# A feed-forward's gate and up products of raw rows, with the norm's factor multiplied in behind them

## The chip, the core and the metric

The kernel runs on one core of a Trainium2 chip. Its time is the device time of one execution in microseconds (us). The core has a matrix engine (PE), a vector engine (DVE), a scalar engine (ACT), a general engine (POOL, also called GpSimd) and an engine that issues transfers (SP). Each engine works through its own list of instructions in order and waits at the head of the list for what the next one needs.

## What is computed

One step of a layer with two feed-forwards around a token mixer. The parts that matter here:

```python
def rms_norm(x, g):
    xf = x.astype(F32)
    y = xf * lax.rsqrt(jnp.mean(xf * xf, axis=-1, keepdims=True) + EPS)
    return (y * g.astype(F32)).astype(x.dtype)

def swiglu(x, w1, w2):
    gate, up = jnp.split(x @ w1, 2, axis=-1)
    return (jax.nn.silu(gate) * up) @ w2
...
        x = x + 0.5 * swiglu(rms_norm(x, lp["norm_ffn1"]), lp["ffn1_w1"], lp["ffn1_w2"])
        y, ns = token_mixing(rms_norm(x, lp["norm_mix"]), lp, st, sample)
        x = x + y
        x = x + 0.5 * swiglu(rms_norm(x, lp["norm_ffn2"]), lp["ffn2_w1"], lp["ffn2_w2"])
```

There are 656 columns (16 meta, 512 prompt and 128 sample tokens; 640 in the second feed-forward), 1024 features and 2816 inner features. The norm's factor, one over the root of a column's mean square, is called R. R belongs to a column, so x's products with the weights may be made of rows without R, and multiplied by R afterwards.

## The kernel before

x lies as eight row tiles of 128 features by 656 columns. The inner features are 22 chunks of 128, in groups of 5, 5, 4, 4 and 4. For each chunk the gate's and the up part's products are made, then the chunk's output v; after a group the second weight matrix's products are added to x, one of eight output tiles o after another (`x<-mx,x` or `x<-mm,x` in the trace).

Every 32-bit operand is split in a high and a low part, and each product is made of three (high by high, high by low, low by high). ACT makes the high part of a weight piece (`whi<-wraw`, `whi<-wsum`), DVE the low part (`wlo<-...`): a piece has four tiles of 128x128. A ring of five such pieces (RING) stands between them and the matrix engine; `more` refills it after each product. The raw weights come through two buffers `wraw`.

The first three chunks (CLASSIC) are plain: 8 row tiles x 3 parts x gate and up x 2 column halves are 96 matmuls. Their operands are raw rows: `gained` makes the high and the low part of gain times x. `act` (lines 696 to 705) multiplies the gate's product with R on DVE (`hg<-mm,R`), takes the tanh on ACT, and two more DVE instructions and one of POOL (`row<-hs,R`) make v.

The other 19 chunks go through `chunk7`, which makes a chunk's four blocks of products (gate and up, two column halves) with seven products of 12 matmuls in place of eight, 84 in all, of sums of weight blocks and of sums of rows. The weight sums are four instructions of POOL for each chunk (`wsum<-...`). The sums of rows are made in `sums_in`, of rows that are normalised first (`row<-x,par,R` is x times gain times R), in pieces between chunks 0 to 2. Here the gate's product needs no R. A chunk's products end in four accumulators p1, p5, p6 and p7; DVE adds a first sum u to two of them (`mx<-mx,u`) before further products are added into the same bank. Behind the gate's tanh an instruction of DVE (`hg<-hs,mx`: tanh in SBUF, gate in PSUM) and one product (`row<-hg,up` or `row<-hg,mx`) write v. Then ACT makes v's high part (`f<-row`) and DVE its low part (`f<-row,f`).

R comes from `row_scale`: the sums of squares of x (`acc`), a matmul with ones, ten small DVE instructions (`nrow`, `rsy`, `rsq`), and a matmul that spreads the result over the partitions (`mx<-sqc,nrow`).

A scheduler sets each engine's list from the program's order and from its own picture of when operands are there; the lists are fixed when the kernel is built. All instructions are recorded with the line of one helper, L188, so the names of the tiles tell them apart. Buffer numbers are left out in the trace's names.

Of the kernel before, what the change touches and what calls it, by code (L numbers as in the profile page):

```python
# [24 lines left out]
CLASSIC = 3  # L25
RING = 5
# [201 lines left out]
class Kern:  # L228
# [366 lines left out]
    def sums_in(self, x, gain, c0, n, slots):  # L595


        nc = self.nc
        V, G, S = nc.vector, nc.gpsimd, nc.scalar
        H, E, _ = slots  # L600
        Y, Z, X, Q = self.pairs(H[:8]), self.pairs(H[8:]), self.pairs(E[:8]), self.pairs(E[8:])
        lo_, hi_ = slice(0, n), slice(n, 2 * n)

        def rows(k):
            r = self.row()[:, :2 * n]
            V.scalar_tensor_tensor(r, x[:, k, c0:c0 + 2 * n], self.p(gain, k), self.R[:, c0:c0 + 2 * n],
                                   op0=OP.mult, op1=OP.mult)
            return r

        def split(dst, cols, src):  # L610
            h, l = (t[:, cols] for t in dst)
            S.activation(h, src, AF.Copy)
            V.tensor_tensor(l, src, h.bitcast(F32), OP.subtract)

        both = slice(0, 2 * n)
        for j in range(4):
            a, b, z = rows(j), rows(j + 4), self.row()[:, both]
            V.tensor_tensor(z[:, hi_], b[:, hi_], a[:, hi_], OP.subtract)
            V.tensor_tensor(a[:, hi_], a[:, hi_], a[:, lo_], OP.subtract)
            V.tensor_tensor(z[:, lo_], b[:, hi_], a[:, hi_], OP.subtract)  # L620
            split(Y[j], both, a)
            split(Z[j], both, z)
        yield
        for j in range(4):
            b, q = rows(j + 4), self.row()[:, lo_]
            split(X[j], both, b)
            G.tensor_tensor(q, b[:, lo_], Z[j][0][:, lo_].bitcast(F32), OP.subtract)
            G.tensor_tensor(q, q, Z[j][1][:, lo_].bitcast(F32), OP.subtract)
            split(Q[j // 2], (lo_, hi_)[j % 2], q)
# [1 line left out]
        self.xc = {"11": part(Y, lo_), "t1": part(Y, hi_), "t2": part(Z, lo_), "t3": part(Z, hi_),
                   "21": part(X, lo_), "22": part(X, hi_),
                   "t4": [[t[:, (lo_, hi_)[j % 2]] for t in Q[j // 2]] for j in range(4)]}
        yield
# [1986 lines left out]
```

## Time and profile before

| what | value |
| --- | --- |
| runs | 1557.96, 1564.41 (median), 1564.84 us |
| profiled execution | 1560.96 us, of it a span of 1559.0 us |
| PE busy | 1463.2 us, 94% |
| DVE busy | 1050.1 us, 67% |
| ACT, POOL busy | 601.4, 459.5 us |
| mean granted clock of PE | 0.962 |

The span runs from the first to the last instruction of the profiled execution; busy shares are averages over the whole span. The granted clock is a share of full speed: 1.00 is 2.4 GHz and 0.50 is 1.2 GHz, and a value between them is a stretch with both.

### The profile page before, as it was taken

The page shows a single profiled execution, that of the slowest core. Times are in us where ns is not written, and L with a number is a line of the kernel's source. Part 1 is how long each engine was busy: PE and PEld are TensorE (multiplying, and loading weights), DVE is VectorE, ACT ScalarE, POOL GpSimd, SP SyncE. Part 2 cuts the span into 40 slices and gives each one's busy share as a digit, 9 for nine tenths or more (in the row PEclk, how much of TensorE's full clock was granted, in tenths as well). Part 3 has the DMA queues.
Part 4 walks back from the last instruction along what each step waited for, and adds up shares of the span by engine and source line. Part 5 has one row for each costly group of instructions (what it writes and reads, how often), then busy time and mean ns, then how long its engine had stood idle before and what let it go on. Part 6 is the DMA issues. An engine that isn't in the chain of part 4 may idle for free.

```text
span 1559.0 us, 26349 instructions
## 1 busy us (share of the span) xinstructions
PE 1463.2 (94%) x10171; PEld 1361.9 (87%) x10171; DVE 1050.1 (67%) x2118; ACT 601.4 (39%) x1142; POOL 459.5 (29%) x580
## 2 busy tenths in 40 slices
PE   7789999999999989999987999989989999999996
PEld 7789999999999757878776877789879999999996
DVE  7985857676775266764765555775995775858586
ACT  5343524343453252454423323233442443434351
POOL 3323314141303333222432523411251313131310
PEclk9889999999999998999888999999989999999998
DMA  8122231313124101212367343473013222222221
GB/s 260 36 68 82 72 105 55 109 55 108 55 88 156 59 35 37 82 59 80 109 202 204 97 109 106 126 242 119 28 44 105 75 76 82 82 82 82 82 82 68
DMA packets 106348, 148.14 MB, mean 95 GB/s; under 512 B 20128, under 2 KB 67760, under 8 KB 106224
## 3 DMA queue, kind: packets, MB, share of 16 engines
q1 hardware_dynamic: 103088, 143.99, 29.2%
q10 hardware_dynamic: 3136, 2.47, 0.6%
q8 instruction: 80, 1.31, 0.4%
q14 instruction: 44, 0.36, 0.1%
HBM read 119.88 MB, written 26.56 MB: 94 GB/s over the span
## 4 chain that ended last, share of the span: by engine, by line
PE 76%; DVE 12%; POOL 4%; issue 3%; DMA 3%; ACT 2%; SPq 1%; DVEq 0%; ACTq 0%; POOLq 0%
PE mx L188 59%; PE mm L188 17%; DVE row L188 2%; DVE wlo L188 1%; DVE e L188 1%; DMA r<-in_w_out 1%; DVE x L188 1%; DVE n L188 1%; DVE hg L188 1%; POOL row L188 1%; POOL qh L188 1%; DVE P L188 1%; SPq L188 1%; DVE rsq L188 0%; DVE f L188 0%
## 5 line engine op out<-in xcount | busy, mean ns | idle before, releaser
L188 ACT ACTIVATE whi<-wraw 128x512 fp32r<-128x512 f32 (+2 forms) x260 | 169.4, 653 | 321.7 <-PE mx L188 195.6
L188 PE MATMUL mx<-f,whi 128*128 128x384 f32 (+2 forms) x1220 | 262.5, 309 | 2.1 <-ACT f L188 2.1
L188 POOL TENSOR_TENSOR wsum<-wraw 128x512 f32<-128x512 f32 x76 | 111.6, 1469 | 451.7 <-DMA wraw<-in_f1w 143.1
L188 DVE TENSOR_TENSOR wlo<-wraw,whi 128x512 fp32r<-128x512 f32 (+1 forms) x227 | 193.5, 853 | 62.9 <-ACT whi L188 62.2
L188 PE MATMUL mm<-n,whi 128*128 128x400 f32 (+2 forms) x992 | 206.6, 329 | 3.9 <-DVE raw L188 2.1
L188 PE MATMUL mx<-e,whi 128*128 128x320 f32 (+4 forms) x996 | 187.0, 317 | 13.3 <-ACT e L188 8.4
L188 PEld LDWEIGHTS mx<-f,whi 128*128 128x128 f32 x1220 | 195.6, 189 | 2.3 <-ACT f L188 2.3
L188 PEld LDWEIGHTS mx<-e,whi 128*128 128x128 f32 x996 | 159.0, 193 | 17.5 <-ACT e L188 9.9
L188 PEld LDWEIGHTS mm<-n,whi 128*128 128x128 f32 x992 | 160.5, 196 | 13.1 <-issue 5.3
L188 PE MATMUL mx<-n,whi 128*128 128x320 f32 (+1 forms) x992 | 169.8, 314 | 0.0
L188 ACT ACTIVATE whi<-wsum 128x512 fp32r<-128x512 f32 x152 | 95.7, 629 | 154.4 <-PE mx L188 112.9
L188 PEld LDWEIGHTS mx<-n,whi 128*128 128x128 f32 x992 | 154.5, 191 | 0.2 <-ACT whi L188 0.2
L188 PE MATMUL mx<-f,wlo 128*128 128x384 f32 (+2 forms) x610 | 152.1, 308 | 0.0
L188 DVE TENSOR_TENSOR wlo<-wsum,whi 128x512 fp32r<-128x512 f32 x152 | 110.6, 729 | 54.9 <-ACT whi L188 54.3
L188 PE MATMUL mm<-n,wlo 128*128 128x400 f32 (+1 forms) x496 | 120.7, 325 | 1.0 <-DVE wlo L188 0.6
L188 POOL TENSOR_TENSOR wlo<-wraw,whi 128x1024 fp32r<-128x1024 f32 (+1 forms) x31 | 67.1, 2173 | 147.7 <-ACT whi L188 104.8
L188 PE MATMUL mx<-e,wlo 128*128 128x320 f32 (+4 forms) x498 | 105.1, 316 | 3.9 <-DVE wlo L188 3.9
L188 DVE SCALAR_TENSOR_TENSOR x<-mx,x 128x256 f32<-128x256 f32 (+2 forms) x130 | 60.9, 483 | 62.9 <-PE mx L188 62.2
L188 PEld LDWEIGHTS mx<-f,wlo 128*128 128x128 f32 x610 | 99.8, 189 | 0.0
L188 PE MATMUL mx<-n,wlo 128*128 128x320 f32 (+1 forms) x496 | 94.3, 312 | 0.4 <-DVE wlo L188 0.4
L188 PE MATMUL mm<-f,whi 128*128 128x400 f32 (+1 forms) x284 | 89.0, 330 | 5.8 <-ACT f L188 5.8
L188 PEld LDWEIGHTS mx<-e,wlo 128*128 128x128 f32 x498 | 82.6, 193 | 4.1 <-DVE wlo L188 4.1
(592 smaller groups left out, 2652.2 us busy)
## 6 DMA issues: line engine op xcount, KB each, us to landing
wraw<-in_f2w SPq DMA_DIRECT2D x22, 1024.0 KB, 5.0
wraw<-in_f1w SPq DMA_DIRECT2D x21, 1024.0 KB, 5.0
wraw<-in_w_in SPq DMA_DIRECT2D x24, 512.0 KB, 3.7
wraw<-in_f1w SPq DMA_DIRECT2D x12, 512.0 KB, 3.6
wraw<-in_f2w SPq DMA_DIRECT2D x12, 512.0 KB, 3.6
scr_rw<-kx SPq DMA_DIRECT2D x16, 328.0 KB, 2.8
wraw<-in_f1w SPq DMA_DIRECT2D x8, 640.0 KB, 4.0
wraw<-in_f2w SPq DMA_DIRECT2D x8, 640.0 KB, 3.9
```

What stands on the lines that cost most here:

```text
L188: return f(*a, **k)
```

## The change

All products of both feed-forwards are now made of raw rows (gain times x, without R). Only chunk 0 stays plain (`chunk0`); chunks 1 to 21 go through `chunk7`. The sums of rows are made of raw rows and column half by column half, in the first feed-forward as the row tiles arrive (`halves_of`, `sums_of`), for which the tiles are loaded in the order 0, 4, 1, 5, 2, 6, 3, 7. R is multiplied in behind the products: in `gate`, on DVE, into the gate's product, and in `gated`, on POOL, into v. The ring of weight pieces goes from five to six, the buffers of row tiles from five to four.

```diff
-CLASSIC = 3
-RING = 5
+ROWS = (0, 4, 1, 5, 2, 6, 3, 7)
+RING = 6
...
-        return self.t(self.fv, [128, NT], "row", bufs=5)
+        return self.t(self.fv, [128, NT], "row", bufs=4)
...
+    def halves_of(self, x, gain, k, hs=(0, 1)):
+
+        c0, n = self.half
+        todo = [("2", 0, 2)] if k > 3 and len(hs) == 2 else [(("11", "12", "21", "22")[k // 4 * 2 + h], h, 1) for h in hs]
+        for name, h, w in todo:
+            hi, lo = self.xc[name][k % 4]
+            v, g = x[:, k, c0 + h * n:c0 + (h + w) * n], self.p(gain, k)
+            self.nc.scalar.activation(hi, v, AF.Copy, scale=g)
+            self.nc.vector.scalar_tensor_tensor(lo, v, g, hi.bitcast(F32), op0=OP.mult, op1=OP.subtract)
+
+    def sums_of(self, x, gain, j):
...
+        S.activation(g12, b12, AF.Copy, scale=g)
+        V.scalar_tensor_tensor(m1, b11, g, g12, op0=OP.mult, op1=OP.subtract)
+        V.scalar_tensor_tensor(t2, b22, g4, m1, op0=OP.mult, op1=OP.add)
+        V.scalar_tensor_tensor(t3, b22, g4, g12, op0=OP.mult, op1=OP.subtract)
+        t4 = g12
+        V.scalar_tensor_tensor(t4, b21, g4, t2, op0=OP.mult, op1=OP.subtract)
+        for name, v, s in (("t23", b[:, :2 * n], 1.0), ("t1", m1, -1.0), ("t4", t4, 1.0)):
+            hi, lo = self.xc[name][j]
+            S.activation(hi, v, AF.Copy, scale=s)
+            V.scalar_tensor_tensor(lo, v, s, hi.bitcast(F32), op0=OP.mult, op1=OP.subtract)
...
-        def gate(pg):
...
-            S.activation(s, pg, AF.Tanh, scale=0.5)
-            V.scalar_tensor_tensor(g, s, 1.0, pg, op0=OP.add, op1=OP.mult)
-            return g
...
-        V.tensor_tensor(v[:, c0 + n:c0 + 2 * n], gate(p5), up1, OP.mult)
+        self.gated(v, self.gate(p5, 1), up1, 1)
...
-        V.tensor_tensor(v[:, c0:c0 + n], g0, p7, OP.mult)
+        self.gated(v, g0, p7, 0)
...
+    def gate(self, pg, h):
+
+        c0, n = self.half
+        g, s = (self.t(self.fv, [128, 328], t, bufs=2)[:, :n] for t in ("hg", "hs"))
+        self.nc.vector.tensor_tensor(g, pg, self.R[:, c0 + h * n:c0 + (h + 1) * n], OP.mult)
+        self.nc.scalar.activation(s, g, AF.Tanh, scale=0.5)
+        self.nc.vector.scalar_tensor_tensor(g, s, 1.0, g, op0=OP.add, op1=OP.mult)
+        return g
+
+    def gated(self, v, g, pu, h):
+        c0, n = self.half
+        c = slice(c0 + h * n, c0 + (h + 1) * n)
+        self.nc.vector.tensor_tensor(g, g, pu, OP.mult)
+        self.nc.gpsimd.tensor_tensor(v[:, c], g, self.R[:, c], OP.mult)
```

The lists of the engines show what the diff alone doesn't. In the list of PE in the opening of the first feed-forward, `mx<-one,acc` is the matmul of the sums of squares, `mx<-sqc,nrow` the one that spreads R, and whi and wlo are pieces of chunk 0 or 1. Before, with chunk 1 plain, fifteen matmuls of it stand ahead of R's; the last of them and what follows:

```order
L188 MATMUL mm100_435<-e421_109,whi69_339 128x256
L188 MATMUL mm100_435<-e522_110,whi69_339 128x256
L188 MATMUL mm100_435<-e421_109,wlo70_340 128x256
L188 MATMUL mx79_358<-sqc_68,nrow66_308 128x16
L188 MATMUL mx79_358<-sqc_68,nrow66_308 128x128 x3
L188 MATMUL mx80_364<-sqc_68,nrow66_308 128x128 x2
L188 MATMUL mx99_434<-f635_126,whi51_184 128x400
L188 MATMUL mx99_434<-f736_127,whi51_184 128x400
```

Now, where `mm101` is one product of chunk 1 (12 matmuls, the last of them shown) and `mx100` the next:

```order
L188 MATMUL mm101_461<-n1213_98,wlo66_261 128x328
L188 MATMUL mm101_461<-n1415_100,wlo66_261 128x328
L188 MATMUL mx79_377<-one_72,acc39_130 16x1
L188 MATMUL mx79_377<-one_72,acc39_130 128x1 x5
L188 MATMUL mx92_432<-sqc_68,nrow80_384 128x16
L188 MATMUL mx92_432<-sqc_68,nrow80_384 128x128 x3
L188 MATMUL mx93_438<-sqc_68,nrow80_384 128x128 x2
L188 MATMUL mx100_460<-n01_86,whi63_256 128x328
L188 MATMUL mx100_460<-n23_88,whi63_256 128x328
L188 MATMUL mx100_460<-n45_90,whi63_256 128x328
```

Chunk 1's other 72 matmuls, which need no R, have moved behind both of the norm's matmuls, and the matmul of the squares behind chunk 0.

In DVE's list of a chunk in the steady part, from the gate to the weight pieces of the next chunk, stood:

```order
L188 SCALAR_TENSOR_TENSOR hg344_1825<-hs343_1824,mx322_1724 128x328
L188 TENSOR_TENSOR wlo350_1850<-wsum333_1779,whi349_1849 128x512
L188 SCALAR_TENSOR_TENSOR hg348_1845<-hs347_1844,mx325_1727 128x328
L188 TENSOR_TENSOR row321_1723<-hg348_1845,up1340_1806 128x328
L188 TENSOR_TENSOR row321_1723<-hg344_1825,mx324_1726 128x328
L188 TENSOR_TENSOR wlo352_1867<-wraw300_1628,whi351_1866 128x512
L188 TENSOR_TENSOR f534_125<-row321_1723,f433_124 128x656
L188 TENSOR_TENSOR wlo360_1892<-wsum336_1782,whi359_1891 128x512
L188 TENSOR_TENSOR u2361_1907<-mx355_1874,c1358_1889 128x328
L188 TENSOR_TENSOR wlo363_1910<-wraw300_1628,whi362_1909 128x512
L188 TENSOR_TENSOR mm356_1875<-mm356_1875,u2361_1907 128x328
L188 TENSOR_TENSOR wlo370_1937<-wraw332_1777,whi369_1936 128x512
```

and now stands:

```order
L188 TENSOR_TENSOR hg365_1881<-mx343_1763,R91_431 128x328
L188 TENSOR_TENSOR wlo368_1889<-wraw316_1643,whi367_1888 128x512
L188 SCALAR_TENSOR_TENSOR hg365_1881<-hs366_1882,hg365_1881 128x328
L188 TENSOR_TENSOR hg365_1881<-hg365_1881,up1358_1842 128x328
L188 TENSOR_TENSOR hg361_1860<-hg361_1860,mx342_1762 128x328
L188 TENSOR_TENSOR wlo370_1907<-wsum352_1801,whi369_1906 128x512
L188 TENSOR_TENSOR f534_125<-row339_1759,f433_124 128x656
L188 TENSOR_TENSOR wlo378_1932<-wraw316_1643,whi377_1931 128x512
L188 TENSOR_TENSOR u2379_1947<-mx373_1914,c1376_1929 128x328
L188 TENSOR_TENSOR wlo386_1960<-wraw348_1796,whi385_1959 128x512
L188 TENSOR_TENSOR mm374_1915<-mm374_1915,u2379_1947 128x328
L188 TENSOR_TENSOR wlo388_1977<-wsum382_1952,whi387_1976 128x512
```

The product with R (`hg<-mx,R`) is new, the instruction behind the tanh reads `hg` in SBUF where it read the gate in PSUM, and the low part of the output (`f534`) stands where it did, but now behind POOL's writing of `row339` and not behind DVE's own.

POOL's list of such a chunk was four weight sums:

```order
L188 TENSOR_TENSOR wsum365_1928<-wraw332_1777 128x512
L188 TENSOR_TENSOR wsum366_1929<-wsum365_1928,wraw332_1777 128x512
L188 TENSOR_TENSOR wsum367_1930<-wraw332_1777 128x512
L188 TENSOR_TENSOR wsum368_1931<-wraw332_1777,wsum366_1929 128x512
```

and is now, for the same chunk with its two products:

```order
L188 TENSOR_TENSOR wsum381_1951<-wraw348_1796 128x512
L188 TENSOR_TENSOR wsum382_1952<-wsum381_1951,wraw348_1796 128x512
L188 TENSOR_TENSOR wsum383_1953<-wraw348_1796 128x512
L188 TENSOR_TENSOR row339_1759<-hg365_1881,R91_431 128x328
L188 TENSOR_TENSOR row339_1759<-hg361_1860,R91_431 128x328
L188 TENSOR_TENSOR wsum384_1954<-wraw348_1796,wsum382_1952 128x512
```

Both products have moved in behind three of the four sums.

In the opening of the second feed-forward, the head of the norm's chain (`nrow<-mx`) stood in DVE's list right behind the raw halves (`f72`, `e12`, ... with x2 and the gain `par`):

```order
L188 SCALAR_TENSOR_TENSOR e52400_11804<-x2_10620,par_69,e42399_11803 128x256
L188 SCALAR_TENSOR_TENSOR e72402_11806<-x2_10620,par_69,e62401_11805 128x256
L188 SCALAR_TENSOR_TENSOR e92404_11808<-x2_10620,par_69,e82403_11807 128x256
L188 SCALAR_TENSOR_TENSOR e112406_11810<-x2_10620,par_69,e102405_11809 128x256
L188 TENSOR_SCALAR nrow2437_11918<-mx2436_11912 128x5
L188 TENSOR_SCALAR rsy2438_11920<-nrow2437_11918 128x5
```

and now stands behind the last of the sums of rows:

```order
L188 SCALAR_TENSOR_TENSOR n72402_11870<-row2458_12025,n62401_11869 128x320
L188 SCALAR_TENSOR_TENSOR row2458_12025<-x2_10712,par_69,row2459_12026 128x320
L188 SCALAR_TENSOR_TENSOR n152410_11878<-row2459_12026,n142409_11877 128x640
L188 SCALAR_TENSOR_TENSOR e112422_11902<-row2458_12025,e102421_11901 128x320
L188 TENSOR_SCALAR nrow2467_12074<-mx2466_12068 128x5
L188 TENSOR_SCALAR rsy2468_12076<-nrow2467_12074 128x5
```

The chain itself is the same; 24 rows of sums have moved in ahead of it.

## Rows read from the trace of the kernel before

**Rows 1.** Page: busy time of each engine; the chain that ended last, by engine.

```profile
PE 1463.2 (94%) x10171; PEld 1361.9 (87%) x10171; DVE 1050.1 (67%) x2118; ACT 601.4 (39%) x1142; POOL 459.5 (29%) x580
...
PE 76%; DVE 12%; POOL 4%; issue 3%; DMA 3%; ACT 2%; SPq 1%; DVEq 0%; ACTq 0%; POOLq 0%
```

**Rows 2.** Stretches: each engine's busy time and instructions, granted clock, DMA share, GB/s.

```profile
48.00:52.00 4.00, 0.00 (x0) 0.00 (x0) 4.00 (x7) 1.84 (x4) 0.00 (x0) 1.00 0.00 0
80.00:84.00 4.00, 2.15 (x8) 1.66 (x8) 4.00 (x4) 1.72 (x3) 3.86 (x3) 0.50 0.00 0
117.00:156.00 39.00, 39.00 (x262) 38.99 (x261) 21.61 (x37) 12.81 (x23) 15.40 (x11) 1.00 0.23 82
173.00:186.00 13.00, 13.00 (x88) 12.98 (x88) 12.22 (x18) 6.88 (x14) 5.71 (x4) 1.00 0.23 83
186.00:199.00 13.00, 12.86 (x86) 12.60 (x85) 9.46 (x19) 6.65 (x13) 0.00 (x0) 1.00 0.27 78
```

**Rows 3.** DVE in order of time: start, us, instruction, idle before it and its releaser.

```profile
179.37 0.48 DVE L188 TENSOR_TENSOR row<-hg,mx 128x328 f32<-128x328 f32 x1
...
181.08 1.93 DVE L188 TENSOR_TENSOR f<-row,f 128x656 fp32r<-128x656 f32 x1
182.93 0.68 DVE L188 TENSOR_TENSOR wlo<-wsum,whi 128x512 fp32r<-128x512 f32 x1
183.53 0.48 DVE L188 TENSOR_TENSOR u<-mx,c 128x328 f32<-128x328 f32 x1
183.94 1.65 DVE L188 TENSOR_TENSOR wlo<-wraw,whi 128x512 fp32r<-128x512 f32 x1
...
187.13 0.49 DVE L188 TENSOR_TENSOR mx<-mx,u 128x328 f32<-128x328 f32 x1
```

**Rows 4.** POOL in order of time, weight sums of the first feed-forward.

```profile
150.57 1.29 POOL L188 TENSOR_TENSOR wsum<-wraw 128x512 f32<-128x512 f32 x1 [5.76 <-DVE wlo L188]
...
177.81 1.28 POOL L188 TENSOR_TENSOR wsum<-wraw 128x512 f32<-128x512 f32 x1 [5.76 <-DMA wraw<-in_f1w]
...
180.57 1.74 POOL L188 TENSOR_TENSOR wsum<-wraw 128x512 f32<-128x512 f32 x1
...
263.67 1.77 POOL L188 TENSOR_TENSOR wsum<-wraw 128x512 f32<-128x512 f32 x1 [5.68 <-DMA wraw<-in_f1w]
```

**Rows 5.** ACT in order of time: copies of one product in two neighbouring chunks.

```profile
173.19 0.43 ACT L188 ACTIVATE c<-mx 128x328 f32<-128x328 f32 x1
...
185.81 0.43 ACT L188 ACTIVATE c<-mx 128x328 f32<-128x328 f32 x1
```

**Rows 6.** DVE groups by form, 120 to 460 us: busy, mean ns, idle before.

```profile
L188 DVE TENSOR_TENSOR row<-hg,up 128x328 f32<-128x328 f32 x17 | 14.1, 829 | 0.6
...
L188 DVE SCALAR_TENSOR_TENSOR hg<-hs,mx 128x328 f32<-128x328 f32 x26 | 12.7, 488 | 0.0
...
L188 DVE TENSOR_TENSOR row<-hg,mx 128x328 f32<-128x328 f32 x9 | 4.4, 489 | 0.4
```

**Rows 7.** DVE in order of time, opening of the first feed-forward.

```profile
5.81 0.90 DVE L188 SCALAR_TENSOR_TENSOR f<-x,par,f 128x656 fp32r<-128x656 f32 x1 [4.56 <-ACT f L188]
...
9.16 2.00 DVE L188 SCALAR_TENSOR_TENSOR e<-x,par,e 128x656 fp32r<-128x656 f32 x1 [1.09 <-ACT e L188]
...
30.39 0.57 DVE L188 TENSOR_TENSOR hg<-mm,R 128x400 f32<-128x400 f32 x1 [0.47 <-ACT R L188]
...
109.54 0.57 DVE L188 SCALAR_TENSOR_TENSOR x<-mx,x 128x400 f32<-128x400 f32 x1
```

**Rows 8.** POOL in order of time, same opening.

```profile
65.87 2.22 POOL L188 TENSOR_TENSOR row<-hs,R 128x400 f32<-128x400 f32 x2 [0.91 <-DVE hs L188]
```

**Rows 9.** DVE in order of time, opening of the second feed-forward.

```profile
1096.34 0.16 DVE L188 TENSOR_SCALAR nrow<-mx 128x5 f32<-128x5 f32 x1
...
1098.15 0.16 DVE L188 SCALAR_TENSOR_TENSOR nrow<-rsq,rsy 128x5 f32<-128x5 f32 x1
...
1180.83 0.89 DVE L188 SCALAR_TENSOR_TENSOR x<-mx,x 128x384 f32<-128x384 f32 x2
```

More of the change, by code (lines that the diff above doesn't have):

```diff
@@ L592, in more @@
             self.ring.append(p)
[L595 to L629, printed above, removed]
-        part = lambda ts, c: [[t[:, c] for t in p] for p in ts]
[L631 to L634, printed above, removed]
@@ L636, in chunk7, with operands @@
-    def chunk7(self, v, c0, n):
+    def operands(self, slots, c0, n):
+        H, E, F = slots
+        Y, Z, X, Q, W = (self.pairs(t) for t in (H[:8], H[8:], E[:8], E[8:], F[6:]))
+        lo, hi = slice(0, n), slice(n, 2 * n)
+        part = lambda ts, c: [[t[:, c] for t in p] for p in ts]
+        two = lambda ts: [[t[:, (lo, hi)[j % 2]] for t in ts[j // 2]] for j in range(4)]
+        self.xc = {"11": part(Y, lo), "t1": part(Y, hi), "t23": part(Z, slice(0, 2 * n)), "t2": part(Z, lo),
+                   "t3": part(Z, hi), "2": part(X, slice(0, 2 * n)), "21": part(X, lo), "22": part(X, hi),
+                   "t4": two(Q), "12": two(W)}
+        self.half = c0, n
@@ new lines, in sums_of @@
+    def sums_of(self, x, gain, j):
+        V, S = self.nc.vector, self.nc.scalar
+        c0, n = self.half
+        b11, b12, b21, b22 = (x[:, k, c0 + h * n:c0 + (h + 1) * n] for k in (j, j + 4) for h in range(2))
+        g, g4 = self.p(gain, j), self.p(gain, j + 4)
+        a, b = self.row(), self.row()
+        g12, m1, t2, t3 = a[:, :n], a[:, n:2 * n], b[:, :n], b[:, n:2 * n]
+        S.activation(g12, b12, AF.Copy, scale=g)
[8 more added lines that the diff above has]
+            V.scalar_tensor_tensor(lo, v, s, hi.bitcast(F32), op0=OP.mult, op1=OP.subtract)
@@ new lines, in gated, with chunk0, mm @@
+    def gated(self, v, g, pu, h):
+        c0, n = self.half
+        c = slice(c0 + h * n, c0 + (h + 1) * n)
+        self.nc.vector.tensor_tensor(g, g, pu, OP.mult)
+        self.nc.gpsimd.tensor_tensor(v[:, c], g, self.R[:, c], OP.mult)
+    def chunk0(self, v, scale, rows):
+        T = self.nc.tensor
+        n = self.half[1]
+        pg, pu = ([self.wide()[:, :n] for _ in range(2)] for _ in range(2))
+        ws = [self.take() for _ in range(4)]
+        wg, wu = ([[t[:, k] for t in w] for w in ws[i:i + 2] for k in range(4)] for i in (0, 2))
+        g = scale()
+        first = [True, True]
+        def mm(ps, w, k, h, parts, stop):
+            xh, xl = self.xc[("11", "12", "21", "22")[k // 4 * 2 + h]][k % 4]
+            for i in parts:
+                wt, xt = ((w[k][0], xh), (w[k][0], xl), (w[k][1], xh))[i]
+                T.matmul(ps[h], wt, xt, start=k == 0 and i == 0, stop=stop and i == parts[-1])
+        if rows:
+            for k in ROWS:
+                for p, w in ((pg, wg), (pu, wu)):
+                    for h in range(2):
+                        mm(p, w, k, h, (0, 1), False)
+            for p, w in ((pg, wg), (pu, wu)):
+                for k in ROWS:
+                    for h in range(2):
+                        mm(p, w, k, h, (2,), k == 7)
+                if p is pg:
+                    next(g)
+        else:
+            for h in range(2):
+                for p, w in ((pg, wg), (pu, wu)):
+                    for k in ROWS:
+                        mm(p, w, k, h, (0, 1, 2), k == 7)
+                    if h == 0 and p is pg:
+                        next(g)
+                for _ in g:
+                    pass
+        self.more()
+        for _ in g:
+            pass
+        for h in range(2):
+            self.gated(v, self.gate(pg[h], h), pu[h], h)
@@ L691, in ffn @@
+    def ffn(self, x, cols, scale, F, done=None, norm=None, also=None, rows=True):
         nc = self.nc
         c0 = cols[0][0]
[L693 to L705 removed]
@@ L2499, in last @@
                                                                          x[:, k - 1:k + 1, a:a + n])
[L2501 removed]
+            K.ffn(x, fcols, lambda: K.row_scale(acc, fb, fcols, False), F, norm=last, rows=False)
         pctx.close()
```

89 lines of the change are left out of this document (20 added, 69 removed).

## The prediction

> **What bounds the kernel now.** I read the page first. The matrix engine is busy 94% of the span, and it holds 76% of the chain that ended last; the vector engine (DVE) holds 12% [rows 1]. An average of this kind hides stages, so the stretches come next [rows 2]. From 117 to 156 us the matrix engine is busy for all of 39.00 us: there time is columns. In the opening of the first feed-forward it stands still for all of 48 to 52, and from 80 to 84 it works 2.15 of 4 us at a granted clock of 0.50, its lower level of 1.2 GHz, while DVE is busy 4.00 of 4 in both stretches [rows 2]. So both ends of the argument are there: fewer columns pay in the steady part, and in the opening whatever shortens or reorders DVE's list pays.
>
> The steady part is less free than its 39.00 suggests. In a chunk in which GpSimd (POOL) makes four weight sums, DVE is busy 12.22 of 13.00 us; in the next one, without POOL, 9.46 [rows 2]. The single instructions say where the difference sits. A low part of a weight piece takes 0.68 us alone, with 0.60 to the next start, and 1.65 beside a POOL sum; the low part of the chunk's output takes 1.93 [rows 3]. POOL's sums lie at 177.81 to 182.3 and DVE's long instructions lie in the same time [rows 3, 4]. The grouped rows tell which instructions suffer: `row<-hg,up`, both inputs in SBUF, has a mean of 829 ns; `row<-hg,mx` and `hg<-hs,mx`, one input in PSUM, have 489 and 488, their undisturbed price [rows 6]. A chunk of 84 products lasts 12.62 us on the matrix engine, from the copy at 173.19 to the next at 185.81 [rows 5], or 0.150 us for a product of 328 columns. The link between the two engines is the add `mx<-mx,u` at 187.13 [rows 3]: the product that follows it adds into the same bank, and in 186 to 199 the matrix engine loses 0.14 us, the first time loss of that group [rows 2]. The cover there is thus used up.
>
> **The change, part by part.** *Columns.* Chunks 1 and 2 of both feed-forwards go from 96 products to 84. 12 x 0.150 = 1.80 us a chunk in the first; at 320 columns (0.1465 a product) 1.76 in the second: 7.1 us in all, if the matrix engine is what bounds those chunks. In both openings it isn't, so I work these out as a whole.
>
> *Opening of the first feed-forward.* DVE's list up to the end of the sums of squares is, by the order: 32 instructions of 328 columns (0.41 apart, as from 183.53 to 183.94 [rows 3]), 8 of 656 and 7 adds of 656 (twice that), 7 weight pieces (0.60): 13.1 + 12.3 + 4.2 = 29.6 us. It begins at about 5.4, half a row earlier than the 5.81 of before, and waits about 1.1 for a row, as ahead of 9.16 [rows 7]. POOL's eleven instructions beside it (about 1.4 us each) cost what they cost in the steady chunk: 12.22 for 18 instructions against 9.46 for 19 is 3.3 us for 5.71 us of POOL, 0.57 per us [rows 2], so 9. The sum is 45.1. Then the chain of the norm, ten steps from 1096.34 to 1098.3 in the second feed-forward [rows 9], with a matmul ahead and one behind it about 3.5: 48.6, where now R is used first at 30.39 [rows 7]. Here lies the catch of the order: the matrix engine has the norm's two matmuls ahead of 72 of chunk 1's 84 products, though raw products no longer need the norm. It has done its 108 earlier products by about 38 and stands some 10 us. From 48.6: 72 products 10.8; 2.7 for some twenty of them at the lower clock, where 8 take 2.15 us [rows 2]; three chunks 37.9; 2.5 lost in their weight sums (below); the first output tile 30 x 0.150 = 4.5: 107.0 against the 109.54 of now [rows 7]. I take **-2.5**. Bounds: no cost from POOL and 3 us less standing, -7; POOL's instructions at the 1.1 us extra of the 2.00 us row at 9.16 [rows 7] and six late weight pieces, +8.
>
> *Opening of the second.* Two weight pieces that wait for POOL stand ahead of the raw halves on DVE, until about 1090.5. Then 16 halves 6.6, sums 24 x 0.41 + 4 x 0.82 = 13.1, two POOL sums beside them 1.6: 1111.8. Only behind all the sums comes the chain of the norm, which ran at 1096.34 before [rows 9]; 2.7 for it and the matmuls: 1114.5. The matrix engine, which has the norm between the two halves of chunk 0, stands from about 1103. Then 48 products 7.0, the clock 2.7, four chunks 49.2, weight sums 2.5, an output tile 4.4: 1180.3 against 1180.83 [rows 9]: **-0.5**, with -4 to +6 by the same bounds.
>
> *Steady chunks with weight sums.* Each has new work. DVE: two products of the gate with the norm's factor, one input in PSUM, so 0.41 each as `row<-hg,mx` [rows 6]: 0.82. The two instructions behind the tanh now have both inputs in SBUF; they go from 0.49 towards the 0.83 of `row<-hg,up` [rows 6] where a POOL sum runs: 0.3. POOL: two products of 328; a 400 and a 256 took 2.22 together [rows 8], 1.1 each. And a wait: the low part of the output now follows both POOL products and the copy on the scalar engine. Before, it began 1.71 us after the last product of the gate began (179.37, 181.08 [rows 3]), hidden by one weight piece. Now it is 0.5 + 1.1 + 0.75 = 2.3 where POOL is free. But POOL's own list has three weight sums ahead of the two products. If these end at 182.3, as now, the low part starts at 182.3 + 2.2 + 0.75 = 185.3, 4.2 late; if the sixth weight piece makes the sums a seventh of a chunk (1.8 us) earlier, 2.4 late. What it wins: it no longer runs beside the sums (1.93 down to about 0.85, so 1.1). Behind it on DVE stand four weight pieces and the add at 187.13, for which the matrix engine waits at once. So 2.4 - 1.1 = 1.3 late, less some cover from the earlier sums: I take 1.0 a chunk. Lower bound 0.4 (sums so early that only DVE's added work counts), upper 2.4. The group of five chunks has three of these, with first sums at 150.57, 164 and 177.81; each of the three groups of four has two, as the one with the second at 263.67 [rows 4]: nine in a feed-forward, 18. About 0.5 of each group's first loss is covered, as no loss is seen before 187: 18 x 1.0 - 8 x 0.5 = **+14**, from 3 to 39.
>
> The Trainium skill, "SBUF — State Buffer", section "Who interferes with whom", says that a DVE instruction with two SBUF inputs contends with a GpSimd instruction that reads SBUF, one with at most one such input doesn't, and that the loser of the shared ports waits. The rows of the gate agree, 829 against 489 ns [rows 6]. It speaks against this change, which gives DVE two more such instructions and GpSimd two more readers in each chunk. Taken at its word for the whole length of each of a chunk's six POOL instructions it would cost DVE 7.9 us where 0.57 per us gives 4.5, so 18 x 3.4 = 61 more, 1635; the chunk of now, 3.3 lost for 5.71 us of POOL [rows 2], speaks against so much.
>
> *Start of the second products.* With four chunks in a group, these reach the last chunk's output 18 products (2.7 us) after its end; the new chain (0.5 + 1.1 + 0.75 + 0.85) is 3.2. About 0.4 at six places: **+2.4**, from 0 to 6. The shorter ring of rows and the new scaled copies on the scalar engine I cost at nothing: that engine is busy 6.88 of 13 [rows 2], and a copy that comes late there is counted in the wait above.
>
> The sum: 1560.96 (the profiled execution, 3.5 below the median of the runs, 1564.41) - 2.5 - 0.5 + 14 + 2.4 = 1574.4.
>
> **The rivals.** *The steady loss doesn't come* (26 in 100): POOL's products slip in ahead of the sums' reach, the ring of six pieces carries the matrix engine across, steady +3, no late second products: 1560.96 - 3 + 3 = 1561, no change. For it: the group shows a loss only in its third chunk. Against: DVE is busy 12.22 of 13.00 and gets 1.1 more [rows 2].
>
> *Faster* (18 in 100): one mechanism, the openings. If POOL doesn't slow these column-wise sums, the sums of squares end at 37 to 41, the norm is there when the matrix engine gets to it, and the 7.1 us of columns and part of the idle time come back: -7 and -4, with the steady loss at its lower bound of 3 or under: 1551 to 1553. It decides as soon as the norm's matmul runs before about 43. For it: DVE's list without POOL ends at 36. Against: the 2.00 us at 9.16 [rows 7].
>
> *Worse* (13 in 100): the sums aren't made earlier, both products always queue behind three of them, and 2.4 is lost in each chunk: 1560.96 - 3 + 39 = 1597. For it: the order of POOL's list. Against: the sums wait for a DMA and for the release of a weight buffer, both earlier with a sixth piece. Of these 13 I give 2 to a dearer collision of the two engines, in which every POOL instruction stops DVE for its whole length: another 3.4 a chunk, 1635.
>
> *The sums made on arrival don't free the matrix engine*, because the norm, now behind them, stands ahead of products that don't need it: that is part of the forecast, and its point is the place of the norm's matmul.
>
> **Numbers.** Forecast (43 in 100): 1574, with its own range 1567 to 1588. The wide range takes in the unchanged case, most of the faster one and the lower part of the worse one: 1552 to 1594. I call 0.5%, 8 us, what a measurement of this kernel can tell from nothing. Faster by more: 0.20; within it: 0.27 (the unchanged case and a sliver of the forecast); slower: 0.53.
>
> **What would show it.** The first add of an output tile at 107 and 1180; a stand of the matrix engine of about 10 us before the norm's matmul in both openings; from 160 to 200 us a distance of 13.4 to 13.8 us between the copies that were 12.62 apart, with DVE idle ahead of `f<-row,f`, released by the scalar engine. Copies still 12.6 apart would make the prediction wrong on its largest term; a norm matmul at 40 would on the openings.

## The result, and the profile after

The changed kernel takes 1634.76 us (median of four executions; 1631.09 to 1636.9) against 1564.62 for the kernel before (median of four, one more than the table ahead has): 1.0453 times as long, 95% interval 1.0414 to 1.0491. Its page, the lines that answer to [rows 1]:

```profile
PE 1475.9 (90%) x10123; PEld 1365.1 (83%) x10123; DVE 1084.4 (66%) x2202; ACT 605.5 (37%) x1168; POOL 535.4 (33%) x656
...
PE 60%; DVE 18%; POOL 8%; issue 6%; DMA 5%; ACT 3%; SPq 0%; POOLq 0%; DVEq 0%; ACTq 0%
```

The matrix engine's share of the chain that ended last fell from 76% to 60%; DVE has 18% and POOL 8%. Where the 76.1 us between the two spans lie can be read from a few instructions that stand in both traces: the first and the last add of an output tile to x in each feed-forward, and one add of the mixer's residual (1078.91 us before). In us between them:

| stretch | before | after | difference |
| --- | --- | --- | --- |
| to the first output add, feed-forward 1 | 109.5 | 114.8 | +5.3 |
| from there to its last | 368.3 | 398.6 | +30.3 |
| mixer, to the residual's add | 601.1 | 605.4 | +4.3 |
| from there to the first output add, feed-forward 2 | 101.9 | 108.7 | +6.7 |
| from there to its last | 364.0 | 393.5 | +29.5 |
| rest | 14.2 | 14.2 | 0.0 |

The mixer's lists are the same in both kernels, and it took 597.5 to 615.6 in the profiles of the experiments; I give its 4.3 to no cause. Of the other 71.8, the two steady parts (from the first output add of a feed-forward to its last) lost 59.8. Stretches of the changed kernel (columns as in [rows 2]):

```profile
40.00:44.00 4.00, 0.06 (x1) 0.00 (x0) 4.00 (x5) 1.53 (x3) 3.01 (x2) 1.00 0.00 0
117.00:156.00 39.00, 39.00 (x262) 38.98 (x262) 20.06 (x35) 10.56 (x19) 11.75 (x9) 1.00 0.24 82
280.00:284.00 4.00, 4.00 (x28) 4.00 (x27) 0.00 (x0) 0.00 (x0) 3.92 (x4) 1.00 0.00 0
288.00:292.00 4.00, 2.13 (x11) 1.86 (x10) 4.00 (x9) 1.63 (x4) 0.00 (x0) 0.87 0.48 133
292.00:296.00 4.00, 4.00 (x22) 4.00 (x21) 2.27 (x6) 1.45 (x3) 0.00 (x0) 0.70 0.00 0
```

From 117 to 156 the matrix engine is as full as before. From 280 to 284 DVE and ACT do nothing at all for 4 us, while POOL is busy; the matrix engine still has products then, and pays later: from 288 to 292 it works 2.13 of 4 us. This is the longest such wait. In the opening the matrix engine stands from 40 to 44, DVE working through.

What ACT, DVE and the matrix engine wait for in the steady part of the first feed-forward (115 to 510 us), in all, times, longest:

```profile
ACT f L188 <- POOL row L188: 60.2, 17, 6.7
```

```profile
DVE f L188 <- ACT f L188: 32.2, 17, 6.3
```

```profile
PE mx L188 <- DVE mx L188: 15.0, 12, 1.9
```

DVE in order of time, the chunk that answers to [rows 3]:

```profile
172.21 1.57 DVE L188 SCALAR_TENSOR_TENSOR hg<-hs,hg 128x328 f32<-128x328 f32 x1
173.81 1.47 DVE L188 TENSOR_TENSOR hg<-hg,up 128x328 f32<-128x328 f32 x1
175.20 0.48 DVE L188 TENSOR_TENSOR hg<-hg,mm 128x328 f32<-128x328 f32 x1
175.61 1.37 DVE L188 TENSOR_TENSOR wlo<-wsum,whi 128x512 fp32r<-128x512 f32 x1
179.40 1.13 DVE L188 TENSOR_TENSOR f<-row,f 128x656 fp32r<-128x656 f32 x1 [2.42 <-ACT f L188]
...
183.68 0.50 DVE L188 TENSOR_TENSOR mx<-mx,u 128x328 f32<-128x328 f32 x1
...
194.54 1.13 DVE L188 TENSOR_TENSOR f<-row,f 128x656 fp32r<-128x656 f32 x1 [1.57 <-ACT f L188]
```

the product that waits for the add at 183.68:

```profile
184.23 1.78 PE L188 MATMUL mx<-e,whi 128*128 128x328 f32 x8 [1.89 <-DVE mx L188]
```

and ACT's copies, which answer to [rows 5], with what stands ahead of them:

```profile
178.61 0.75 ACT L188 ACTIVATE f<-row 128x656 fp32r<-128x656 f32 x1 [5.54 <-POOL row L188]
179.27 0.62 ACT L188 ACTIVATE whi<-wraw 128x512 fp32r<-128x512 f32 x1
179.79 0.43 ACT L188 ACTIVATE c<-mx 128x328 f32<-128x328 f32 x1
...
194.94 0.42 ACT L188 ACTIVATE c<-mm 128x328 f32<-128x328 f32 x1
```

The copies are 15.15 us apart where they were 12.62. On DVE two instructions on the way to the output are long here: `hg<-hs,hg` behind the tanh, which now reads SBUF alone, takes 1.57, and the product behind it 1.47; the low part itself fell from 1.93 to 1.13. And the low part waits 2.42 us for ACT's high part, which waits 5.54 for POOL's products; ACT's list holds the next chunk's copy and weight pieces behind it. That wait of DVE stands in nearly every chunk: 1.5 us or more in 42 of the 44. Of POOL's queue nothing much is left: in 41 of the 44 chunks its first product starts 0.1 us after DVE's, and only at 176.4, 283.4 and 1302.8 does it stand behind weight sums (1.1, 4.7, 1.1 us). The chunk and the stretch shown are two of these three.

The openings, DVE in order of time (the rows that answer to [rows 7] and [rows 9]):

```profile
17.33 4.55 DVE L188 SCALAR_TENSOR_TENSOR row<-x,par,row 128x328 f32<-128x328 f32 x3
...
27.68 1.49 DVE L188 SCALAR_TENSOR_TENSOR row<-x,par,row 128x328 f32<-128x328 f32 x3
...
38.34 1.79 DVE L188 TENSOR_TENSOR wlo<-wsum,whi 128x512 fp32r<-128x512 f32 x1
...
52.98 0.22 DVE L188 TENSOR_SCALAR nrow<-mx 16x1 f32<-16x1 f32 x2 [2.17 <-PE mx L188]
...
56.82 0.50 DVE L188 TENSOR_TENSOR hg<-mm,R 128x328 f32<-128x328 f32 x1
...
114.81 0.57 DVE L188 SCALAR_TENSOR_TENSOR x<-mx,x 128x400 f32<-128x400 f32 x1
...
1154.76 0.16 DVE L188 TENSOR_SCALAR nrow<-mx 128x5 f32<-128x5 f32 x1
...
1227.46 0.89 DVE L188 SCALAR_TENSOR_TENSOR x<-mx,x 128x384 f32<-128x384 f32 x2
```

and the matrix engine at the matmul of the squares in the first:

```profile
50.51 2.44 PE L188 MATMUL mx<-one,acc 128*16 128x1 f32 x12 [10.45 <-DVE acc L188]
```

### The profile page after: what moved, and what is told of

It is laid out like the page before. It is cut to its first block, busy times and chain, and to the rows that moved or that the text cites. A ratio compares the mean times of both kernels' runs of the same rounds, so it can differ in the third digit from the quotient of the medians.

```text
span 1635.1 us, 26351 instructions
## 1 busy us (share of the span) xinstructions
PE 1475.9 (90%) x10123; PEld 1365.1 (83%) x10123; DVE 1084.4 (66%) x2202; ACT 605.5 (37%) x1168; POOL 535.4 (33%) x656
## 4 chain that ended last, share of the span: by engine, by line
PE 60%; DVE 18%; POOL 8%; issue 6%; DMA 5%; ACT 3%; SPq 0%; POOLq 0%; DVEq 0%; ACTq 0%
PE mx L188 46%; PE mm L188 13%; DVE wlo L188 4%; POOL row L188 3%; DVE hg L188 3%; DMA wraw<-in_f2w 2%; DVE row L188 1%; DVE mx L188 1%; ACT f L188 1%; POOL wsum L188 1%; DVE f L188 1%; DMA wraw<-in_f1w 1%; DVE n L188 1%; DMA r<-in_w_out 1%; DVE e L188 1%
## 5 line engine op out<-in xcount | busy, mean ns | idle before, releaser
L188 PE MATMUL mx<-f,whi 128*128 128x256 f32 (+4 forms) x1176 | 257.2, 312 | 5.6 <-DVE f L188 3.3
L188 PE MATMUL mm<-n,whi 128*128 128x400 f32 (+2 forms) x1032 | 217.5, 331 | 15.8 <-DVE n L188 6.7
L188 PE MATMUL mx<-e,whi 128*128 128x320 f32 (+1 forms) x896 | 164.5, 323 | 43.1 <-DVE mx L188 42.9
L188 PE MATMUL mx<-n,whi 128*128 128x320 f32 (+1 forms) x1112 | 190.7, 313 | 9.5 <-ACT n L188 9.5
L188 PEld LDWEIGHTS mx<-n,whi 128*128 128x128 f32 x1112 | 172.2, 189 | 9.7 <-ACT n L188 9.7
L188 POOL TENSOR_TENSOR row<-hg,R 128x328 f32<-128x328 f32 (+1 forms) x88 | 93.9, 1087 | 262.3 <-DVE hg L188 234.8
L188 DVE TENSOR_TENSOR wlo<-wsum,whi 128x512 fp32r<-128x512 f32 x168 | 135.2, 816 | 27.3 <-ACT whi L188 27.3
L188 PE MATMUL mx<-f,wlo 128*128 128x384 f32 (+4 forms) x588 | 146.8, 308 | 0.0
L188 PE MATMUL mm<-n,wlo 128*128 128x400 f32 (+2 forms) x516 | 124.7, 323 | 0.4 <-POOL wlo L188 0.4
L188 DVE TENSOR_TENSOR f<-row,f 128x656 fp32r<-128x656 f32 (+1 forms) x44 | 44.3, 1006 | 72.1 <-ACT f L188 72.0
L188 PE MATMUL mx<-e,wlo 128*128 128x320 f32 (+1 forms) x448 | 90.6, 319 | 0.0
```

The source lines that it names most:

```text
L188: return f(*a, **k)
```

## The experiments

Theory L: DVE's add into p5, the matrix engine's last products, the gate on DVE, POOL's products, ACT's high part and DVE's low part follow one another, and the next chunk's add stands behind that low part in DVE's list. So the steps form one serial loop through the engines, from one chunk's add to the next, and each step lengthens the chunk though no engine is full. Rivals: D, DVE's throughput; Q, the queue behind POOL's three sums; C, the collisions of POOL with DVE, which make DVE's instructions longer. Times are medians, with the ratio to the kernel before and its interval. A chunk's length is the distance from one add that writes `up` to the next. Gains are differences of medians; by the ratios some are up to 4 us smaller (22 for experiment 5, 9 for 6, 10 for 10).

**1. The second product by R on DVE.**

```diff
-        self.nc.gpsimd.tensor_tensor(v[:, c], g, self.R[:, c], OP.mult)
+        self.nc.vector.tensor_tensor(v[:, c], g, self.R[:, c], OP.mult)
```

> The changed kernel, with the second product by R made on DVE instead of POOL (same numbers, two instructions of 328 columns per chunk more on DVE, two fewer on POOL). Theory L (a serial loop through the engines: add, last products, gate, POOL's two products, high part, low part, next add, 15.15 us a chunk): the loop loses POOL's 2.2 us and gains about 0.9, so chunks with weight sums come to about 13.6 to 14.0 and the kernel to 1585 to 1605. Rival D (DVE's throughput is what is short): DVE has 0.9 us more, so 1640 to 1655. Rival Q (POOL's products queue behind three weight sums): as L, but the chunk falls to 13.2 or less, 1575 to 1585.

Measured: 1590.73, 1.0171 (1.0154 to 1.0188). The chunks with sums last 13.1 to 14.1. Giving DVE more instructions saves 44 us: D as stated is out, and POOL's step is the larger part of the loss. The edit takes away POOL's wait and POOL's collisions at once, so it doesn't part L from C.

**2. POOL's step alone, in the kernel before.**

```diff
+        def through(g, pu, h):
+            c = slice(c0 + h * n, c0 + (h + 1) * n)
+            V.tensor_tensor(g, g, pu, OP.mult)
+            nc.gpsimd.tensor_tensor(v[:, c], g, self.R[:, c], OP.mult)
...
-        V.tensor_tensor(v[:, c0 + n:c0 + 2 * n], gate(p5), up1, OP.mult)
+        through(gate(p5), up1, 1)
...
-        V.tensor_tensor(v[:, c0:c0 + n], g0, p7, OP.mult)
+        through(g0, p7, 0)
```

> The kernel before, with only POOL's step put into chunks 3 to 21: DVE's products go to a buffer, POOL multiplies them with R into v (R a second time, so the output is not the reference's). Theory L: the loop of 13.0 us gets POOL's 2.2, less 1.0 for a low part that no longer collides: 14.2 or more in chunks with weight sums, 1590 to 1605. Rival D: no DVE work is added, so within 5 us of before, 1560 to 1570. Rival Q: 4.2 us late behind the three sums, 1610 or more.

Measured: 1625.27, 1.0404 (1.0383 to 1.0425): 62 us from one step, more than L gave. With a ring of five, Q does act here. POOL:

```profile
172.00 1.74 POOL L188 TENSOR_TENSOR wsum<-wraw 128x512 f32<-128x512 f32 x1
173.69 1.74 POOL L188 TENSOR_TENSOR row<-hg,R 128x328 f32<-128x328 f32 x2
```

and DVE:

```profile
170.80 0.48 DVE L188 TENSOR_TENSOR hg<-hg,mm 128x328 f32<-128x328 f32 x1
...
176.25 0.84 DVE L188 TENSOR_TENSOR f<-row,f 128x656 fp32r<-128x656 f32 x1 [3.67 <-ACT f L188]
```

DVE's last product is done at 171.3, POOL's first starts at 173.69 behind three sums, and DVE waits 3.67. In 18 of 38 chunks POOL's first product starts 1.1 to 4.1 us after DVE's first is done. What the loop, the queue and the collisions each have of the 62 us this run doesn't part.

**3. The gate's step alone, in the kernel before.**

```diff
-            S.activation(s, pg, AF.Tanh, scale=0.5)
-            V.scalar_tensor_tensor(g, s, 1.0, pg, op0=OP.add, op1=OP.mult)
+            V.tensor_tensor(g, pg, self.R[:, c0 + h * n:c0 + (h + 1) * n], OP.mult)
+            S.activation(s, g, AF.Tanh, scale=0.5)
+            V.scalar_tensor_tensor(g, s, 1.0, g, op0=OP.add, op1=OP.mult)
```

> The kernel before, with only the gate's step put into chunks 3 to 21: DVE multiplies the gate's product with R first, so the two instructions behind the tanh read SBUF alone (the output is not the reference's). Theory L: 0.41 us on the loop and up to 1.1 where a weight sum of POOL runs beside, 13.6 to 14.3 a chunk, 1572 to 1585. Rival D: about as much as the whole of the steady loss, 1610 or more. Rival Q: 1565 to 1572.

Measured: 1578.53, 1.0095 (1.008 to 1.011), 15 us, the smaller part, as L had it; chunks of 13.3 to 13.6, a little under L's.

**4. The changed kernel with five weight pieces** (`RING = 5`, five row buffers).

> The changed kernel with five weight pieces and five row buffers, as before. Theory L and rival Q: no part of the loss, 1630 to 1640. A theory that the ring or the row buffers cost the time: 1600 or less.

Measured: 1664.49, 1.0647 (1.0625 to 1.067). L and Q missed: the sixth piece, with one row buffer less, is worth 30 us. Part of it is the queue of experiment 2, which is back: POOL's first product stands behind weight sums in 8 of the 44 chunks, by 1.1 to 4.1 us, against 3 of 44 in the changed kernel. But these waits make only some 20 us in all, against 7 there; how the rest comes about, and whether the ring or the row buffers cause it, wasn't run.

**5. The output's two parts tied behind the next chunk's add.**

```diff
         V.tensor_tensor(up1, p7, c5, OP.add)
+        if late:
+            k = self.t(self.fv, [128, 1], "kone", bufs=2)
+            V.tensor_scalar(k, up1[:, 0:1], 0.0, 1.0, op0=OP.mult, op1=OP.add)
+            late(k)
...
```

> The changed kernel; the high and the low part of a chunk's output are tied (through a factor of one that is made behind the add) to come after the next chunk's add into p5, the last chunk of a group excepted. All work and POOL's two products stay. Theory L (the serial loop): the way over POOL no longer lies between one add and the next; chunks with weight sums fall from 15.15 us to what DVE needs, 9.1 and some 4.5 of collisions with POOL, 13.4 to 13.8, and the kernel to 1595 to 1610. Rival C (it is the collisions themselves, POOL's six instructions stopping DVE): nothing of them is taken away, 1625 to 1640.

Measured: 1608.88, 1.0312 (1.0271 to 1.0354). The loop is a cause, worth 26 us, but chunks with sums come only to 14.1 to 14.4, not to 13.8. One of them (columns as in [rows 2]):

```profile
181.00:195.24 14.24, 12.85 (x84) 12.58 (x84) 14.21 (x20) 6.36 (x12) 8.73 (x6) 1.00 0.22 71
```

DVE is busy 14.21 of 14.24 us and waits for nothing: now it is its throughput that binds, with 20 instructions beside 8.73 us of POOL. Not all of this is the changed kernel's own need: the tied low part now runs beside the sums, where it takes 1.90 (1.13 before the edit), and the factor of one is an instruction more. 46 us to the kernel before are still missing.

**6. The openings reordered.**

```diff
-                    if i > 3:
-                        K.sums_of(x, "norm_ffn1", i - 4)
+                    K.sumsq(acc0, x[:, i, :], i, 0, NT)
...
                 if p is pg:
                     next(g)
+                    sums()
...
```

> The changed kernel with the openings reordered alone: the sums of squares are made as the row tiles arrive, and the sums of rows are written behind the head of the norm's chain in both feed-forwards. My reading of the openings (the norm stands ahead of raw products and behind all of DVE's sums): the matrix engine goes on at about 42 instead of 57 us and the first output tile comes at 102 to 105 instead of 114.8; the second opening gains 3 to 7: 1617 to 1627. Rival: the matrix engine waits for the sums of rows instead, as long as before: 1630 to 1640.

Measured: 1623.51, 1.0395 (1.036 to 1.0431): the first output adds come 4.2 us earlier in the first feed-forward and 10.6 in the second. The place of the norm was the loss of the second; the first gained less than I said (114.8 to 110.7, not to 102 to 105). There the wait of 10.45 is gone, but R's first use comes only at 51.6, and the matrix engine later waits 3.87 for a low part and 2.69 for an add.

**7. R at the output tiles.**

```diff
-        self.nc.vector.tensor_tensor(g, g, pu, OP.mult)
-        self.nc.gpsimd.tensor_tensor(v[:, c], g, self.R[:, c], OP.mult)
+        self.nc.vector.tensor_tensor(v[:, c], g, pu, OP.mult)
...
-            nc.vector.scalar_tensor_tensor(x[:, o, a:a + n], q[:, :n], 0.25, x[:, o, a:a + n],
-                                           op0=OP.mult, op1=OP.add)
+            t = self.t(self.fv, [128, 400], "xr", bufs=1)[:, :n]
+            nc.vector.scalar_tensor_tensor(t, q[:, :n], 0.25, self.R[:, a:a + n], op0=OP.mult, op1=OP.mult)
+            nc.vector.tensor_tensor(x[:, o, a:a + n], x[:, o, a:a + n], t, OP.add)
```

> The changed kernel, with the second factor R moved from v to the output tiles: DVE writes v directly, as in the kernel before, and adds (0.25 R times product) to x with two instructions instead of one. Theory L: no POOL in the loop, only the gate's step is left: 13.0 to 13.4 a chunk with weight sums, the openings as in the changed kernel: 1572 to 1582. Rival: the output phases, with 16 more instructions of DVE for a group, become longer by more than 1 us each: 1585 or more.

Measured: 1583.26, 1.0138 (1.0098 to 1.0178): between the two. The chunks of a group of four gain 6 to 9 us, the output phases lose 0.8 to 1.7 each, so the rival holds for a part; and chunks with sums come only to 13.7 to 14.1 where they follow one another, not to 13.4, so L's forecast for them was too low.

**8. Experiments 1 and 5 together.**

> The product by R on DVE (as in the first experiment, 1590.7) and the two parts of the output behind the next add. Theory L: the loop is already short there, so what is left is DVE's own need, about 9.9 and 3.3 of collisions, 13.2 against 13.6 a chunk: 1580 to 1588. Rival C: no difference from 1590.

Measured: 1579.08, 1.0111 (1.008 to 1.0141), against C's 1590; chunks with sums 13.6 to 14.1, not 13.2. Against experiment 5 the same step on DVE gains 30 us though the low part no longer stands in the way of the next add. The last chunk of each group isn't tied, so its wait for POOL is part of the 30; what else can be in it are the collisions, and the next experiment looks at those alone.

**9. As 8, with POOL's two products made once more for nobody.**

```diff
         self.nc.vector.tensor_tensor(v[:, c], g, self.R[:, c], OP.mult)
+        d = self.t(self.fv, [128, 328], "spare", bufs=1)[:, :n]
+        self.nc.gpsimd.tensor_tensor(d, g, self.R[:, c], OP.mult)
```

> The kernel of the eighth experiment (product by R on DVE, the output's parts behind the next add, 1579.1) with POOL making the same two products once more into a spare buffer that nothing reads. Nothing waits for POOL's result, so only what POOL's two instructions take from DVE is added. Theory C for the half that the loop doesn't explain (collisions): DVE loses about 1 us a chunk and chunks with weight sums go from 13.7 to 14.5 or more, 1592 to 1602. Rival (the delays are waits for POOL's result, not collisions): 1577 to 1583.

Measured: 1632.72, 1.0459 (1.0406 to 1.0513), 54 us for two instructions whose result nobody reads: in the direction of C, and 30 us over the range that I had for it. POOL and DVE beside each other:

```profile
189.92 1.76 POOL L188 TENSOR_TENSOR wsum<-wsum,wraw 128x512 f32<-128x512 f32 x1
...
195.04 2.21 POOL L188 TENSOR_TENSOR spare<-hg,R 128x328 f32<-128x328 f32 x2 [1.85 <-DVE hg L188]
```

```profile
190.46 1.57 DVE L188 SCALAR_TENSOR_TENSOR hg<-hs,hg 128x328 f32<-128x328 f32 x1
191.96 0.48 DVE L188 TENSOR_TENSOR hg<-mx,R 128x328 f32<-128x328 f32 x1
...
194.89 1.61 DVE L188 TENSOR_TENSOR row<-hg,R 128x328 f32<-128x328 f32 x2
196.42 1.38 DVE L188 TENSOR_TENSOR wlo<-wsum,whi 128x512 fp32r<-128x512 f32 x1
```

DVE's products by R in the two kernels, 120 to 510 us (busy, mean ns, idle before), first experiment 8, then this one:

```profile
L188 DVE TENSOR_TENSOR row<-hg,R 128x328 f32<-128x328 f32 x34 | 15.4, 493 | 0.0
```

```profile
L188 DVE TENSOR_TENSOR row<-hg,R 128x328 f32<-128x328 f32 x34 | 29.3, 902 | 0.0
```

Chunks with sums go from 13.7 to 15.1 us: 1.4 for 2.2 us of POOL. `hg<-mx,R`, one input in PSUM, stays at 0.48 beside a weight sum; `hg<-hs,hg` before it takes 1.57, and a weight piece beside the spare products 1.38. DVE waits for POOL nowhere in the two feed-forwards, so the 1.4 isn't a wait for a buffer that POOL still reads. My range counted chunks with sums alone. The third chunk of a group of four, which has none, went from between 12.5 and 12.8 us to between 14.3 and 16.8, the openings lost 4.6 and 4.7, and in the two feed-forwards the granted clock fell to half at ten places where it didn't in experiment 8, 3.4 us each. So C is shown, and with experiment 8 it holds for the half that L doesn't explain.

**10. The last chunk of each group on DVE.**

```diff
-        self.nc.gpsimd.tensor_tensor(v[:, c], g, self.R[:, c], OP.mult)
+        (self.nc.vector if self.ends else self.nc.gpsimd).tensor_tensor(v[:, c], g, self.R[:, c], OP.mult)
...
+                self.ends = i == kk - 1
```

> The changed kernel, with the second product by R on DVE in the last chunk of each group alone. It prices what the output products' start costs: if they wait for the last chunk's way over POOL, the last chunk and what follows it shorten by 0.7 to 1.4 us at ten places, 1622 to 1629 against 1635. If that way is hidden by the 18 products that don't need it, as my forecast had it but for 0.4: 1631 to 1637.

Measured: 1622.2, 1.0391 (1.0353 to 1.0429). The last chunks of the groups and the start of the output products, for which I had forecast 2.4, cost 12.6 us; the collision in these chunks, which this edit also takes away, wasn't run apart.

**11. Experiments 6 and 8 together.**

> The openings of the sixth experiment and the chunks of the eighth together. If the two causes add: 1579.1 less the 11.5 of the openings, 1565 to 1571, no more than the kernel before by 0.5%. If the openings' gain was idle time that DVE's relief gives back anyway: 1574 to 1580.

Measured: 1563.28, 1.0011 (0.9988 to 1.0034): the causes add, and the kernel before is reached. The openings give 15.8 us here, 4 more than alone, which is within the noise of the two. So the 71.5 us from the changed kernel to this one fall in three steps: 26 by untying the low part (experiment 5), 30 by taking the product by R off POOL (8), 16 by the openings.

**12. Openings of 6, parts as in 5, R at the output tiles with POOL's add.**

```diff
...
-        self.nc.vector.tensor_tensor(g, g, pu, OP.mult)
-        self.nc.gpsimd.tensor_tensor(v[:, c], g, self.R[:, c], OP.mult)
+        self.nc.vector.tensor_tensor(v[:, c], g, pu, OP.mult)
...
-            nc.vector.scalar_tensor_tensor(x[:, o, a:a + n], q[:, :n], 0.25, x[:, o, a:a + n],
-                                           op0=OP.mult, op1=OP.add)
+            t = self.t(self.fv, [128, 400], "hg", bufs=2)[:, :n]
+            nc.vector.scalar_tensor_tensor(t, q[:, :n], 0.25, self.R[:, a:a + n], op0=OP.mult, op1=OP.mult)
+            (nc.vector if last else nc.gpsimd).tensor_tensor(x[:, o, a:a + n], x[:, o, a:a + n], t, OP.add)
```

> The openings of the sixth experiment, the output's parts behind the next add, and R multiplied in at the output tiles: DVE multiplies the product by 0.25 R, POOL adds it to x (DVE in the last group). In chunks neither engine has a second product by R. If DVE's need in chunks with weight sums (then about 12.9) and the openings set the time: 1550 to 1560, under the kernel before. If POOL's adds collide with DVE's weight pieces in the output phases as its products did in the chunks: 1562 to 1575.

Measured: 1549.83, 0.9918 (0.9889 to 0.9946): faster than both kernels, the kernel before by 0.8%. Two of its stretches:

```profile
117.00:156.00 39.00, 39.00 (x263) 39.00 (x262) 25.46 (x41) 13.18 (x24) 26.05 (x22) 1.00 0.23 73
160.00:173.00 13.00, 13.00 (x89) 12.99 (x88) 12.97 (x20) 6.35 (x12) 5.62 (x5) 1.00 0.23 81
```

In a chunk with weight sums DVE is busy 12.97 of 13.00 us and the matrix engine doesn't wait; in the output phase shown POOL works 26.05 of 39 us, and the matrix engine is full there too. Of the 11.4 us between this profile's span and that of the kernel before, 3.6 lie in the mixer, which no edit touches.

## Why the prediction was wrong

Forecast were 1574, with 1552 to 1594 as the wide range; measured were 1634.76. The sign and the place of the largest loss were right. The step that failed is the term for **steady chunks with weight sums**, forecast at +14 with an upper end of 39, together with the **start of the second products**, forecast at +2.4: the two steady parts measured +30.3 and +29.5, 59.8 in all. Four things in it were off.

*The price of POOL's products for DVE.* I added 1.1 us to DVE's list (0.82 and 0.3) and counted POOL's two new products only as a wait, at nothing for what they make DVE lose. Experiment 9 shows that they take 1.4 us of DVE in a chunk when nobody waits for them, more than the 0.82 that DVE needs to make them itself. I had the rate for it, 0.57 per us of POOL, and used it in the openings; here it would have given 1.3. In experiment 5, where the wait is mostly gone, DVE is full for 14.2 us a chunk, over the matrix engine's 12.62; some of that is the edit's own low part beside the sums, and whether another order of the lists would need less wasn't run.

*The wait.* I took it from POOL's queue: 2.4 us late behind three sums. In the changed kernel that queue is nearly gone (3 of 44 chunks): the third sum ends about when DVE's first product does. With a ring of five it acts (experiments 2 and 4). Whether the sums came earlier by more than I allowed, or DVE's product came later, these runs don't part. In its place stands the loop: 26 us by experiment 5. I had its parts (0.5, 1.1, 0.75), but took their sum, 2.3, as hidden where POOL is free. It isn't: from the start of DVE's last product to the low part there are 3.1 to 3.2 us in most chunks, as POOL's first product begins only when DVE's first is done and the two take 2.2; DVE idles 1.5 us or more in 42 of 44 chunks. Nor had I the 1.57 and 1.47 us instructions ahead of it.

*How far a late chunk reaches.* I counted 18 chunks, two in a group of four. The third chunk of such a group was late too, 14.23 to 15.67 us in the first feed-forward (12.39 before), though it has no sums; and the last chunks with the start of the output products cost 12.6 us (experiment 10).

*The clock.* I priced its fall in the openings alone. Of the 30.3 us, 19.9 are waits in the matrix engine's list. After three of the four longest of these, 1.9 us each, the granted clock fell to half in the first feed-forward; the stretches 288 to 296 show one of them, 1.87 us without work and then a mean clock of 0.87 and 0.70. Some 3.4 us at half cost 1.7 each time, 5.1 in all; the other 5 of the 30.3 I can't place. In the second feed-forward's steady part it fell once, after a wait of 2.40, and not after four others of 2.15 to 2.29.

The **openings** came out at +5.3 and +6.7, not -2.5 and -0.5. The reason given was right: the matrix engine waited 10.45 us at the matmul of the squares and 10.42 for the norm in the second, R's first use came at 56.82 (I had 48.6 for the norm), and in the second the norm's chain began behind the last sum at 1154.76, which is 1114.9 less the shift of 39.9 that the kernel had there, against 1111.8. Off was the size. In the first, the sums of squares ended at 50.45 and not at 45.1: three sums of rows beside POOL took 4.55 us, three without it 1.49, and four of the weight pieces among the squares took over 1.7. And from there to R's first use it took 6.4 us where I had 3.5, with other small instructions of DVE between the steps. Experiment 6 gives 11.3 us of the whole time back by the order alone, though in the first opening less than the stand of 10.45.

The rival in which every POOL instruction stops DVE for its whole length gave 1635. That is the time that was measured, but it is luck, since it didn't come that way: the rival asked for the forecast's 1.0 us and 3.4 more in each of 18 chunks, where a chunk lost 2.5 (15.15 against 12.62), with the rest in the third chunks, the outputs' starts and the openings; and experiment 9 has 0.64 us of DVE per us of POOL, not one. Which instructions collide, the rule of the Trainium skill ("SBUF — State Buffer", section "Who interferes with whom") told rightly: 1.57 us for `hg<-hs,hg` against 0.48 for `hg<-mx,R`. The rival of no steady loss and the faster one are out. So is the worse one as it was told, with both products always behind three sums: in the changed kernel they stood there in 3 of 44 chunks.

What stays open: the mixer's 4.3 us, how the sixth weight piece gives its 30 us, and how much of experiment 12's gain is owed to each of its three parts; they weren't run apart.

## What to carry to other kernels

Work moved to a second engine isn't free for the first when both read the same memory: here two products cost DVE 1.4 us on POOL and 0.82 on itself. Price an added instruction on every engine's list that it runs beside, and on the loop from one iteration to the next, before asking who queues for it. And a factor that belongs to a column can go where engines are idle: at the output tiles, with POOL's add, the matrix engine lost nothing in the phase shown (experiment 12).

## What the runs showed that I had not expected

The depth of the weight ring matters to a queue on another engine: 30 us lie between five pieces and six, with one row buffer more or less, and the queue is a part of them (experiment 4 against the changed kernel). And two POOL instructions in a chunk whose result nobody reads made the kernel 54 us slower (experiment 9), by what DVE lost beside them, in chunks without weight sums too, and by falls of the clock behind it.
